# Mixing the second GLA pair's decay levels with its own value and gate projections, and moving half of a key load behind the first attention block

## The chip, the cores and the metric

One Trainium2 chip, one core of it. The metric is the device time of one execution in microseconds (us), median of several; lower is better. The engines are TensorE (PE), VectorE (DVE), ScalarE (ACT), GpSimd (POOL) and SyncE (SP), which issues nearly all DMAs here. "Clock" is the share of full speed that the chip granted to TensorE.

## The reference, cut to what matters

One layer for 1024 tokens of width 1024: an FFN, a mixer, an FFN, each with a residual and a layer norm. The mixer is what the change touches. It projects the tokens once and splits the columns into head groups:

```python
proj = h @ w_in
gq, gk, gv, gg, ga, dq, dk, dv, iq, ik, iw = jnp.split(proj, offs, axis=-1)
...
log_a = (jax.nn.log_sigmoid((ga @ w_gla_a2 + b_gla_a)) / GLA_TAU)
o = gla_chunked(q, k, v, log_a)          # 4 heads, linear attention with decay
o = o * lax.rsqrt(jnp.mean(o * o, axis=-1, keepdims=True) + RMS_EPS) * gla_norm_g
o_gla = o.reshape(B, T, GLA_WIDTH) * jax.nn.silu(gg)
o_dsa = dsa_attention(dq, dk, dv, iq, ik, iw)   # 8 heads, the 256 best keys of an index score
return jnp.concatenate([o_gla, o_dsa], axis=-1) @ w_out
```

In `gla_chunked` each step multiplies a running state by `exp` of a cumulated decay, adds `k^T v`, and reads it with `q`. In `dsa_attention` an index score picks, for each query, at most 256 of the keys before it; softmax attention runs over those.

## The kernel before, in words

The FFNs take most of the time and stay as they are. Each float32 matmul of a projection is three fast ones (high times high, low times high, high times low), so one projection block of 128x512 is 24 matmuls: 3 for each of 8 slices of the width.

**The GLA pairs.** The four GLA heads are worked on in two pairs by the generator `gla_pair` (L868 to L1052), which gives control back after each piece of work. A pair first makes `pz`, the decay's logits (two halves of 512 tokens), takes log-sigmoid of them on ACT and DVE (`az`, `kz`, the tiles `mz` are the tiles `kz`), and cumulates along 128-token blocks with scans on DVE (`bT`, L898). Then, for each half `i` of the tokens, it computes the state of the blocks (`turned_keys`: `pk`, `kt`; `pkv`, then `state`) and the scores inside a block by levels L = 0, 64, 32, ... 1 (L957): level 0 is the diagonal (`qk = gk*gq` on POOL into `kz[1]`, L964, then `pd` on PE); every other level builds `ee` (DVE, then Abs and Exp on ACT), `kz` (POOL) and `qz` (DVE), a small product `pa` on PE (L995), and copies it into `at` through a mask on DVE (L1006). `po` = `at` times values plus `qe` times state closes the half; `og` is `po` with norm and gate, and goes to DRAM.

**Its inputs.** `gla_items(p)` projects `gq`, `gk` (4 blocks of 24 matmuls, tile `pf`) and `gv`, `gg` (8 token blocks, tile `pt`, by `proj_tok`), takes silu of the gate and multiplies it by the norm's weights (`gg*gn`, L1452, on POOL). `dq_steps` projects the queries of the other attention: two halves of the tokens by four units; after each unit `stage_split` (L1393) splits the block into a high and a low part (`part`, ACT and DVE) and sends both to DRAM (`q_hi`, `q_lo`).

**Order.** Inside `in_order()` the PE instructions stand as the code writes them; all other engines are ordered by the framework's scheduler, which moves work up. Before the change, pair 1's `gq`, `gk`, `gv` and `gg` blocks all run in one piece between the first `pz` and the levels, and only the queries' steps are mixed with the levels, three steps (9 matmuls) a level.

**The search and the attention.** While this goes on, DVE is ending the search for the 256th key and turns scores into biases (`search_keys`, L781; `keep_keys`, L816 to L848). The tiles that hold the split tokens of the first half are then overwritten by the keys: `kst` (`xl`, `xh`), eight DMAs of 512 KB (L1525), and the values `vt` (L1526). They can start only once the queries of the first half (i = 0) have been projected. Queries come back from DRAM into `qq` and `ql` (`load_q`, L1063). `attend` starts with three `lg` (logits, L1091); `rb` (L1150) closes a 128-token block. `Weights.need` brings weights ahead, RING = 6 of them.

Of the kernel before, what the change touches and what calls it, by code (L numbers as in the profile page):

```python
# [7 lines left out]
F32 = mybir.dt.float32  # L8
# [107 lines left out]
class Block:  # L116
# [542 lines left out]

    def proj_tok(self, u, b, xT):  # L660

        nc = self.nc
        cols = slice((b % 4) * P, (b % 4) * P + P)
        xh, xl = xT[0][b // 4], xT[1][b // 4]
        pt = self.ps_pj.tile([P, 512], F32, tag="pj", name=self.uid("pt"))
        for k in range(KD):
            wh, wl = self.w.get(u + k // 2)
            nc.tensor.matmul(pt, xh[:, k, cols], wh[:, k % 2, :], start=(k == 0), stop=False)  # L668
            nc.tensor.matmul(pt, xh[:, k, cols], wl[:, k % 2, :], start=False, stop=False)  # L669
            nc.tensor.matmul(pt, xl[:, k, cols], wh[:, k % 2, :], start=False, stop=(k == KD - 1))  # L670
        return pt

# [199 lines left out]
    def gla_pair(self, p, g, gp, go, sgp, ps, masks, consts, o_dram):  # L872
# [32 lines left out]
                )  # L905
        yield
        gq, gk, gv, gg = g[p]
        ebl = gp.tile([P, NB], F32, tag="ebl", name=self.uid("ebl"), bufs=2)
        nc.scalar.activation(ebl, bT.rearrange("p (b t) -> p b t", t=P)[:, :, P - 1], AF.Exp, scale=1.0 / 16)

# [17 lines left out]
            nc.scalar.activation(kt, pk, AF.Copy)  # L928
            return kt

        kt = turned_keys(0)
        yield
        state = None
        for i in range(2):
            ts = slice(i * HT, (i + 1) * HT)
            last = NB - 1 - 4 * i
            pkv = self.ps_tp.tile([P, 4, P], F32, tag="tp", name=self.uid("pkv"))
            for j in range(min(4, last)):
                for h in range(2):
# [1 line left out]
                    nc.tensor.matmul(  # L941
                        pkv[rows, j, :], kt[:, j, rows], gv[:, 4 * i + j, h * P : (h + 1) * P], start=True, stop=True
                    )
            states = [state]
            for j in range(min(4, last)):
                b = 4 * i + j
                new = gp.tile([P, P], F32, tag="state", name=self.uid("state"), bufs=5)
                if b == 0:
                    V.tensor_copy(new, pkv[:, j, :])
                else:  # L950
                    V.scalar_tensor_tensor(new, state, ebl[:, b : b + 1], pkv[:, j, :], ALU.mult, ALU.add)
                state = new
                states.append(new)
            yield
            at = go.tile([P, 4, 2, P], F32, tag="at", name=self.uid("at"), bufs=1)
            for step, L in enumerate((0, 64, 32, 16, 8, 4, 2, 1)):
                if L == 8:  # L957
                    eb = gp.tile([P, HT], F32, tag="ee", name=self.uid("eb"), bufs=2)
                    nc.scalar.activation(eb, bT[:, ts], AF.Exp, scale=1.0 / 16)
                    V.tensor_mul(qe[0][:HP], gq[:HP, ts], eb[:HP])  # L960
                    nc.gpsimd.tensor_mul(qe[1][HP:], gq[HP:, ts], eb[HP:])
# [40 lines left out]
                for h in range(2):  # L1002
                    if L == HP:
                        nc.scalar.activation(at[:HP, :, h, HP:], pa[h][:HP], AF.Copy)
                    else:
# [2 lines left out]
                            masks[L].unsqueeze(1).to_broadcast([P, 4, HP // L, L]),  # L1008
                            pa[h].rearrange("p a (n l) -> p a n l", l=L),
                        )  # L1010
                yield
            if i == 0:
                kt = turned_keys(1)
                yield
            if p == 1 and i == 1:
                po = [self.ps_pj.tile([P, 4, P], F32, tag="pj", name=self.uid("po")) for _ in range(2)]
# [159 lines left out]
    def run(self):  # L1176
# [160 lines left out]
        with ExitStack() as s2:  # L1337
# [8 lines left out]
            with ExitStack() as s3:  # L1346
# [84 lines left out]
                def gla_items(p):  # L1431
                    gq = gqk.tile([P, T], F32, tag="gq", name=f"gq{p}", bufs=1)
                    gk = gqk.tile([P, T], F32, tag="gk", name=f"gk{p}", bufs=1)
                    for dst, u, sc in ((gq, um["gq", p], 0.125), (gk, um["gk", p], 1.0)):
                        self.w.need(u, u)
                        for i in range(2):
                            pt = self.proj_feat(u, i, x1T)
                            nc.scalar.activation(dst[:, i * HT : (i + 1) * HT], pt, AF.Copy, scale=sc)
                            yield
                    gv = go.tile([P, NB, 256], F32, tag="gv", name=f"gv{p}", bufs=1)  # L1440
                    gg = go.tile([P, NB, 256], F32, tag="gg", name=f"gg{p}", bufs=1)
                    u = um["gvg", p]
                    self.w.need(u, u + 3)
                    for b in range(NB):
                        pt = self.proj_tok(u, b, x1T)
                        nc.scalar.activation(gv[:, b, :], pt[:, 0:256], AF.Copy)
                        nc.scalar.activation(gg[:, b, :], pt[:, 256:512], AF.Copy)
                        yield
                    nc.scalar.activation(gg, gg, AF.Silu)
                    for b in range(0, NB, 2):  # L1450
                        gv2 = gg[:, b : b + 2, :].rearrange("p b (h f) -> p (b h) f", h=2)
                        nc.gpsimd.tensor_mul(gv2, gv2, gn.unsqueeze(1).to_broadcast([P, 4, P]))  # L1452
                    g_in[p] = (gq, gk, gv, gg)

                def dv_items():
                    u = um["dv"]
# [7 lines left out]
                def dq_steps():  # L1464
                    for i in range(2):
                        for t, u in enumerate(um["dq"]):
                            for pt in self.proj_steps(u, i, x1T):
                                yield
                            stage_split(pt, q_dram, t, i)

                def gla(p):
                    return self.gla_pair(p, g_in, gp, go, sgp, ps, masks, consts, og_dram)

                for _ in gla_items(0):
                    pass
                self.interleave(dv_items(), gla(0), 3)
                items = gla_items(1)
                for _ in range(4):
                    next(items)
                side = gla(1)  # L1480
                next(side)
                for _ in items:
                    pass
                self.w.need(um["dq"][0], um["dq"][3])
                fill = dq_steps()
                half = (3, 2) + (3,) * 7
                with self.in_order():
                    for n in (3, *half, 3, 0, 0, 0, 0, *half):
                        next(side)
                        for _ in range(n):  # L1490
                            next(fill)
                    for _ in fill:
                        pass
                    for _ in side:
                        pass
                found = self.search_keys(scores, bp, tkp, tp)
                for b in scores:
                    bias[b] = self.keep_keys(
# [17 lines left out]
                qp.append((qq, ql))  # L1516
                self.load_q(i, q_dram, qp[i])
            vt = [p.tile([P, 4, 512], F32, name=f"vt{i}") for i, p in enumerate((vp0, vp))]
            for i in range(2):
                cs = slice(i * HT, (i + 1) * HT)  # L1520
                for e in range(2):
                    for j in range(2):
                        r0 = 64 * (e ^ j)
                        src = k_dram[i][j].rearrange("(q e d) t -> e d q t", e=2, d=64)
                        nc.sync.dma_start(kst[e][r0 : r0 + 64, :, cs].bitcast(F32), src[e])  # L1525
                nc.sync.dma_start(vt[i], dv_dram[i].rearrange("(b t) f -> t b f", t=P))  # L1526
            c0 = self.new_half(1)
            cat = []
            with tc.tile_pool(name="ps_att", bufs=1, space=PSUM, reuse_waits="tile") as ps:
                def begin(b):  # L1530
                    c = catp.tile([P, D], F32, tag="cat", name=self.uid("cat"))
                    cat.append(c)
                    nc.sync.dma_start(c[:, 0:512], og_dram[b * P : (b + 1) * P, :])
                    return c

                def end(b, c):
                    if b < 4:
                        self.split_cat(c, b, [[c0[0]], [c0[1]]])
                    if 0 < b < 5:
                        if b == 1:  # L1540
                            self.w.need(um["out"][0], um["out"][0] + 3)
                        half = x1_dram[(b - 1) * P : b * P, 0:512]
                        xh = scores[NB - 1][:, 512:]
                        nc.sync.dma_start(xh, half)
                        pt = self.proj_tok(um["out"][0], b - 1, [[c0[0]], [c0[1]]])
                        nc.vector.scalar_tensor_tensor(xh, xh, ALPHA, pt, ALU.mult, ALU.add)
                        nc.sync.dma_start(half, xh)

                self.attend(kst, vt, bias, q_dram, qp, ep, tp, rp, ps, begin, end)
# [114 lines left out]
```

## Time and profile before

| | before |
|---|---|
| median of 3 runs | 2028.18 us (2027.34 to 2028.61) |
| profiled execution | 2028.19 us, of which span 2026.1 us |
| PE busy | 1957.7 us (97%) |
| DVE, ACT, POOL busy | 1474.1, 823.0, 594.3 us (73, 41, 29%) |
| clock, mean | 0.985 |

The span is first to last instruction; the profiled execution's time has 2.1 us around it. PE is busy nearly always, so what can be won are its few gaps and its stretches at a low clock. The work that the change moves lies between 970 and 1150 us.

### The profile page before, as it was taken

What the parts mean: (1) busy time and instruction counts of PE and PEld (TensorE: products, weight loads), DVE (VectorE), ACT (ScalarE), POOL (GpSimd) and SP (SyncE); (2) the same over time, 40 slices, a digit from 0 to 9 for tenths busy, and PEclk for the clock granted to TensorE, in tenths of its full rate; (3) what the DMA queues carried; (4) which work ended last, traced back from release to release, by engine and by line L of the source; (5) the groups of instructions that cost most, each with busy time, mean ns of one, the idle gap of its engine ahead of it and who ended that gap; (6) DMA issues with size and microseconds to landing.
All of it is one profiled execution on the core that took longest, in us unless ns stands there. A gap on an engine that the chain in (4) does not pass through costs nothing.

```text
span 2026.1 us, 26935 instructions
## 1 busy us (share of the span) xinstructions
PE 1957.7 (97%) x9752; PEld 1608.2 (79%) x9752; DVE 1474.1 (73%) x2326; ACT 823.0 (41%) x1319; POOL 594.3 (29%) x503
## 2 busy tenths in 40 slices
PE   8999999999999999999988899999999999999997
PEld 6888888888888788777766678787888888888886
DVE  5577778785668767899974457576677877866577
ACT  4333332334333454798433346333333233234331
POOL 3345445440001102144253000044444544420011
PEclk9999999999999999999988899999999999999999
DMA  5345445469656332021127621432453454487664
GB/s 176 115 141 188 147 144 182 155 207 331 193 181 205 105 93 84 22 63 57 49 68 174 171 72 38 141 133 71 145 176 132 160 183 136 156 288 264 207 194 149
DMA packets 192708, 298.43 MB, mean 147 GB/s; under 512 B 16304, under 2 KB 98368, under 8 KB 192576
## 3 DMA queue, kind: packets, MB, share of 16 engines
q1 hardware_dynamic: 192576, 296.72, 45.2%
q8 instruction: 76, 1.25, 0.3%
q14 instruction: 56, 0.46, 0.1%
HBM read 205.96 MB, written 90.70 MB: 146 GB/s over the span
## 4 chain that ended last, share of the span: by engine, by line
PE 80%; DVE 8%; issue 3%; DMA 3%; ACT 2%; POOL 2%; SPq 1%; POOLq 0%; DVEq 0%; ACTq 0%
PE pd L491 19%; PE pq L320 14%; PE pq L321 14%; PE pq L319 14%; DVE junk L781 3%; PE pf L655 3%; PE pf L656 3%; PE pf L657 2%; PE pv L1134 2%; PE tpe L1118 2%; PE pt L668 1%; PE pt L670 1%; PE pt L669 1%; PE tp L265 1%; POOL wlo L75 1%
## 5 line engine op out<-in xcount | busy, mean ns | idle before, releaser
L97 DVE TENSOR_TENSOR wloq<-rw,whiq 128x512 fp32r<-128x512 f32 (+1 forms) x208 | 213.9, 1031 | 113.2 <-ACT whiq L96 112.2
L97 DVE TENSOR_TENSOR wlod<-rd,whid 128x1024 fp32r<-128x1024 f32 x154 | 186.2, 1219 | 127.2 <-ACT whid L96 126.6
L96 ACT ACTIVATE whid<-rd 128x1024 fp32r<-128x1024 f32 x154 | 160.9, 1058 | 242.5 <-PE pd L491 170.9
L96 ACT ACTIVATE whiq<-rw 128x512 fp32r<-128x512 f32 (+1 forms) x208 | 163.5, 806 | 227.3 <-POOL rw L305 95.6
L491 PE MATMUL pd<-wlod,whid 128*128 128x512 f32 x616 | 239.7, 389 | 0.8 <-DVE wlod L97 0.8
L491 PE MATMUL pd<-whid,wlod 128*128 128x512 f32 x616 | 239.2, 389 | 0.0
L491 PE MATMUL pd<-whid 128*128 128x512 f32 x616 | 234.7, 390 | 0.0
L319 PE MATMUL pq<-b_h,whiq 128*128 128x512 f32 x576 | 228.7, 397 | 1.9 <-ACT b_h L96 1.9
L320 PE MATMUL pq<-b_l,whiq 128*128 128x512 f32 x576 | 225.0, 391 | 1.2 <-DVE b_l L97 1.2
L321 PE MATMUL pq<-b_h,wloq 128*128 128x512 f32 x576 | 224.8, 391 | 0.0
L207 POOL TENSOR_TENSOR rs<-ve,neghalf 128x1 f32<-128x1 f32 x24 | 33.8, 1410 | 609.4 <-DVE ve L225 609.4
L431 ACT ACTIVATE c<-c 128x512 f32<-128x512 f32 x80 | 50.5, 632 | 236.5 <-DVE c L355 134.5
L319 PE MATMUL pq<-xh,whiq 128*128 128x512 f32 x352 | 137.7, 391 | 0.0
L321 PE MATMUL pq<-xh,wloq 128*128 128x512 f32 x352 | 137.0, 389 | 0.0
L320 PE MATMUL pq<-xl,whiq 128*128 128x512 f32 x352 | 136.9, 389 | 0.0
L491 PEld LDWEIGHTS pd<-wlod,whid 128*128 128x128 f32 x616 | 115.7, 188 | 25.4 <-DVE wlod L97 1.6
L491 PEld LDWEIGHTS pd<-whid,wlod 128*128 128x128 f32 x616 | 115.6, 188 | 24.2
L491 PEld LDWEIGHTS pd<-whid 128*128 128x128 f32 x616 | 115.6, 188 | 23.8 <-ACT whid L96 0.4
L668 PE MATMUL pt<-whi,xh 128*128 128x512 f32 x320 | 129.6, 405 | 4.4 <-ACT stage L1460 2.4
L319 PEld LDWEIGHTS pq<-b_h,whiq 128*128 128x128 f32 x576 | 108.6, 189 | 23.8 <-ACT b_h L96 2.5
L320 PEld LDWEIGHTS pq<-b_l,whiq 128*128 128x128 f32 x576 | 108.7, 189 | 23.2 <-DVE b_l L97 2.1
L669 PE MATMUL pt<-wlo,xh 128*128 128x512 f32 x320 | 126.8, 397 | 0.0
(263 smaller groups left out, 4498.4 us busy)
## 6 DMA issues: line engine op xcount, KB each, us to landing
rw<-in_ffn_w_gu_dram SPq DMA_DIRECT2D x88, 512.0 KB, 4.2
rd<-h_dram SPq DMA_DIRECT2D x154, 256.0 KB, 3.4
h_dram<-c SPq DMA_DIRECT2D x148, 256.0 KB, 3.0
rt<-in_ffn_w_down_dram SPq DMA_DIRECT2D x44, 512.0 KB, 3.5
t_dram<-rt SPq DMA_DIRECT2D x44, 512.0 KB, 3.0
rd<-t_dram SPq DMA_DIRECT2D x88, 256.0 KB, 3.8
rd<-in_ffn_w_down_dram SPq DMA_DIRECT2D x66, 256.0 KB, 3.8
raw<-in_w_in_dram SPq DMA_DIRECT2D x20, 512.0 KB, 3.8
```

The source lines that it names most:

```text
L96: self.nc.scalar.activation(hi, src, AF.Copy)
L97: self.nc.vector.tensor_sub(lo, src, hi)
L319: mm(bank, wh[:, k, :], xh[:, k, :], start=(start and k == 0), stop=False)
L320: mm(bank, wh[:, k, :], xl[:, k, :], start=False, stop=False)
L321: mm(bank, wl[:, k, :], xh[:, k, :], start=False, stop=(stop and k == 3))
L431: nc.scalar.activation(t, t, AF.Silu)
L491: nc.tensor.matmul(bank, left, right, start=(i == 0 and n == 0), stop=(i == ng - 1 and n == 2))
L655: nc.tensor.matmul(pt[:m], wh[:, k, :m], xh[:, k, :], start=(k == 0), stop=False)
L656: nc.tensor.matmul(pt[:m], wh[:, k, :m], xl[:, k, :], start=False, stop=False)
L668: nc.tensor.matmul(pt, xh[:, k, cols], wh[:, k % 2, :], start=(k == 0), stop=False)
L669: nc.tensor.matmul(pt, xh[:, k, cols], wl[:, k % 2, :], start=False, stop=False)
L781: V.tensor_scalar(junk[:, :n], scores[b], thr, None, ALU.is_ge, ALU.add, accum_out=cnt)
```

## The change

Six edits:
1. `proj_tok` becomes a generator `tok_steps` that gives control back after each of the 8 slices. The 8 `gvg` blocks of pair 1 become 64 steps that stand ahead of the queries' 64 steps in one list of filler; the levels take 14 steps, then 6 each (second half: 7 each), and what is left (8 steps, the last unit of the queries) comes behind the last `po`.
2. In pair 1 the keys are turned at level 4 and the states made at level 2 of each half, not ahead of the levels.
3. `gv`/`gg` weights come with a shorter ring (4), and those of the queries one by one.
4. `gg*gn` of pair 1 goes from POOL to DVE.
5. Weights of the output projection are asked for at the start of block 0 of the attention rather than at the end of block 1.
6. The second half of keys and values is loaded in `begin` of block 1 (`load_keys(1)`), not ahead of the attention.

```diff
+    def tok_steps(self, u, b, xT):
...
-        return pt
+            yield pt
...
-        kt = turned_keys(0)
-        yield
-        state = None
+        for i in range(2):
+            ts = slice(i * HT, (i + 1) * HT)
+            if not p:
+                kt = turned_keys(i)
+                yield
+                states_of(i, kt)
+                yield
             for step, L in enumerate((0, 64, 32, 16, 8, 4, 2, 1)):
+                if p and L == 4:
+                    kt = turned_keys(i)
...
+                if p and L == 2:
+                    states_of(i, kt)
                 yield
...
-                    self.w.need(u, u + 3)
+                    self.w.need(u, u + 3, RING - 2 * p)
                     for b in range(NB):
-                        pt = self.proj_tok(u, b, x1T)
+                        if p and b in (4, 6):
+                            self.w.need(u + b // 2 + 2, u + b // 2 + 2, 1)
+                        for k, pt in enumerate(self.tok_steps(u, b, x1T)):
+                            if k < KD - 1:
+                                yield
...
-                        nc.gpsimd.tensor_mul(gv2, gv2, gn.unsqueeze(1).to_broadcast([P, 4, P]))
+                        (nc.vector if p else nc.gpsimd).tensor_mul(gv2, gv2, gn.unsqueeze(1).to_broadcast([P, 4, P]))
...
+                side = gla(1)
+                next(side)
                 items = gla_items(1)
                 for _ in range(4):
                     next(items)
-                side = gla(1)
-                next(side)
-                for _ in items:
-                    pass
-                self.w.need(um["dq"][0], um["dq"][3])
-                fill = dq_steps()
-                half = (3, 2) + (3,) * 7
+                def fill():
+                    yield from items
+                    yield from dq_steps()
+                fill = fill()
                 with self.in_order():
-                    for n in (3, *half, 3, 0, 0, 0, 0, *half):
+                    for n in (14,) + (6,) * 7 + (8, 0, 0, 0) + (7,) * 8:
                         next(side)
                         for _ in range(n):
                             next(fill)
-                    for _ in fill:
-                        pass
                     for _ in side:
                         pass
+                for _ in fill:
+                    pass
...
+            load_keys(0)
...
+                    if b == 0:
+                        self.w.need(um["out"][0], um["out"][0] + 3)
+                    if b == 1:
+                        load_keys(1)
```

How it moves instructions, at three places. On PE at the start of pair 1 before the change: behind the two `pz` follow 192 `pt` matmuls and then `pk`, `pkv` and `pd`; `pf` are queries here.

```order
L882 MATMUL pz_7881<-mT,wa_5343 128x512
L882 MATMUL pz_7885<-mT,wa_5343 128x512
L668 MATMUL pt_7914<-whi_7726,xh_3620 128x512
L669 MATMUL pt_7914<-wlo_7727,xh_3620 128x512
L670 MATMUL pt_7914<-whi_7726,xl_3621 128x512
L668 MATMUL pt_7914<-whi_7726,xh_3620 128x512
```

The same place after the change; `pf_7879` is the last block of `gk`, and `pt_7915` the first of the eight value and gate blocks.

```order
L655 MATMUL pf_7879<-xh_3622,whi_7042 128x512
L656 MATMUL pf_7879<-xl_3623,whi_7042 128x512
L657 MATMUL pf_7879<-xh_3622,wlo_7043 128x512
L886 MATMUL pz_7730<-mT,wa_5343 128x512
L977 MATMUL pd_7909<-heads,kz_6648 128x2 x4
L672 MATMUL pt_7915<-whi_7753,xh_3620 128x512
L673 MATMUL pt_7915<-wlo_7754,xh_3620 128x512
L674 MATMUL pt_7915<-whi_7753,xl_3621 128x512
```

The diagonal product `pd`, which reads `kz_6648`, now stands directly behind the second `pz`, and every `pt` behind it.

On DVE at the end of `keep_keys` before the change: the last rows of the last block (`score_6535`) stand together, and the states and the diagonal follow.

```order
L821 SCALAR_TENSOR_TENSOR keep_9528<-keep_9528,left_9532 128x1024
L822 TENSOR_SCALAR keep_9528<-score_6535,search_8875 128x1024
L823 TENSOR_TENSOR keep_9528<-keep_9528 128x1024
L825 TENSOR_SCALAR score_6535<-keep_9528 128x1024
L920 TENSOR_TENSOR mT<-bT_7878 128x512
L949 COPY state_8201<-pkv_8192 128x128
```

The same place after the change: level work of the first half stands between, down to the masked copies of level 1 (`mask_101`), which are the last that the first `po` needs.

```order
L826 TENSOR_SCALAR keep_9510<-score_6535,search_8857 128x1024
L1016 COPY_PREDICATED at_8347<-mask_105,pa_8172 128x4x32x2
L827 TENSOR_TENSOR keep_9510<-keep_9510 128x1024
L1016 COPY_PREDICATED at_8347<-mask_105,pa_8173 128x4x32x2
L999 TENSOR_TENSOR qz_6645<-gq_7748,ee_8441 128x256
L829 TENSOR_SCALAR score_6535<-keep_9510 128x1024
L951 COPY state_8193<-pkv_8184 128x128
L991 TENSOR_TENSOR ee_8487<-bT_7723 128x512
L953 SCALAR_TENSOR_TENSOR state_8195<-state_8193,ebl_7905,pkv_8184 128x128
L953 SCALAR_TENSOR_TENSOR state_8197<-state_8195,ebl_7905,pkv_8184 128x128
L953 SCALAR_TENSOR_TENSOR state_8199<-state_8197,ebl_7905,pkv_8184 128x128
L1016 COPY_PREDICATED at_8347<-mask_101,pa_8237 128x4x64
```

So the whole first half's level work moved up among the rows of `keep_keys`.

On SP after the change, at the key loads (`k_hi_85` and `k_lo_86` are the first half of the tokens, `k_hi_87` and `k_lo_88` the second; `q_hi_83` is the first part of the second half's queries):

```order
L1545 DMA xh_9560<-k_lo_86 64x4x512
L1545 DMA xl_9561<-k_lo_86 64x4x512
L1545 DMA xh_9560<-k_hi_87 64x4x512
L1545 DMA xh_9560<-k_lo_88 64x4x512
L1545 DMA xl_9561<-k_hi_87 64x4x512
L1546 DMA vt_9578<-dv_dram_89 128x4x512
L1545 DMA xl_9561<-k_lo_88 64x4x512
L1407 DMA q_hi_83<-part_8625 128x512
L1407 DMA q_lo_84<-part_8626 128x512
L1072 DMA qq_9562<-q_hi_81 64x8x128
L1073 DMA ql_9563<-q_lo_82 64x4x128
```

All eight key loads still stand ahead of the first `qq` and `ql`, as they did before the change. The first `vt`, which stood behind that `ql`, now stands among them.

## Rows read from the trace of the kernel before

**Rows 1.** The page: its first line, and the chain that ended last.

```profile
span 2026.1 us, 26935 instructions
...
PE 80%; DVE 8%; issue 3%; DMA 3%; ACT 2%; POOL 2%; SPq 1%; POOLq 0%; DVEq 0%; ACTq 0%
```

**Rows 2.** Busy time by stretch: length, PE, PEld, DVE, ACT, POOL, clock, DMA share, GB/s.

```profile
1000.00:1040.00 40.00, 38.80 (x187) 31.28 (x185) 39.15 (x58) 15.55 (x27) 13.08 (x12) 1.00 0.03 8
1040.00:1050.00 10.00, 0.83 (x12) 0.50 (x12) 4.29 (x7) 3.75 (x5) 10.00 (x11) 0.68 0.45 157
1050.00:1076.00 26.00, 26.00 (x182) 20.47 (x180) 16.39 (x29) 11.27 (x20) 11.64 (x14) 0.93 0.24 82
...
1122.00:1146.00 24.00, 14.75 (x77) 11.74 (x77) 9.80 (x48) 9.32 (x41) 3.06 (x4) 0.72 0.59 167
```

**Rows 3.** PE's timeline: start, length, instruction, idle time before it and its releaser.

```profile
974.60 0.61 PE L1027 MATMUL po<-state,qe 128*128 128x128 f32 x4
...
984.71 1.98 PE L882 MATMUL pz<-mT,wa 16*128 16x512 f32 x4
...
1049.50 1.12 PE L995 MATMUL pa<-qz,kz 64*64 64x64 f32 x16 [9.17 <-POOL kz L988]
...
1076.37 0.39 PE L657 MATMUL pf<-xh,wlo 128*128 128x512 f32 x1
...
1103.07 0.79 PE L655 MATMUL pf<-xh,whi 128*128 128x512 f32 x1 [5.70 <-DVE part L1396]
...
1121.94 0.28 PE L1091 MATMUL lg<-xh,qq 128*128 128x256 f32 x1
...
1124.87 0.49 PE L1024 MATMUL po<-gv,at 128*128 128x128 f32 x2 [2.06 <-DVE part L1396]
...
1136.86 0.55 PE L1091 MATMUL lg<-xh,qq 128*128 128x256 f32 x1 [4.37 <-DVE mx L1095]
...
1146.25 1.07 PE L1150 MATMUL rb<-ident,rc 128*64 128x128 f32 x8
```

**Rows 4.** Timelines of DVE, POOL and ACT around pair 1's setup.

```profile
995.99 2.62 DVE L898 TENSOR_TENSOR_SCAN bT<-onesf,kz 128x128 f32<-128x128 f32 x8
...
1039.46 1.77 DVE L920 TENSOR_TENSOR mT<-bT 128x512 f32<-128x512 f32 x1
...
998.76 1.32 POOL L964 TENSOR_TENSOR kz<-gk,gq 128x512 f32<-128x512 f32 x1 [9.14 <-DVE bT L898]
...
1039.22 5.59 POOL L1452 TENSOR_TENSOR gg<-gg,gn 128x512 f32<-128x512 f32 x4
...
988.47 1.28 ACT L895 ACT_TABLE_LOAD   x1
```

**Rows 5.** DVE's groups of instructions, 1050 to 1100: busy, mean ns, idle before.

```profile
L1006 DVE COPY_PREDICATED at<-mask,pa 128x256 f32<-128x256 uint8 x14 | 6.5, 532 | 3.8 <-PE pa L995 3.8
L981 DVE TENSOR_TENSOR ee<-bT 128x512 f32<-128x512 f32 x9 | 6.2, 691 | 3.8 <-POOL qe L961 2.0 <-POOL kz L988 1.2
L989 DVE TENSOR_TENSOR qz<-gq,ee 128x256 f32<-128x256 f32 x9 | 5.1, 564 | 0.5 <-ACT ee L983 0.5
...
L960 DVE TENSOR_TENSOR qe<-gq,eb 64x512 f32<-64x512 f32 x2 | 1.9, 947 | 4.1 <-ACT eb L959 4.1
L970 DVE TENSOR_TENSOR at<-ident,pd 128x1024 f32<-128x1024 f32 x1 | 1.2, 1207 | 0.0
L951 DVE SCALAR_TENSOR_TENSOR state<-state,ebl,pkv 128x128 f32<-128x128 f32 x3 | 1.0, 346 | 7.0 <-PE pkv L941 7.0
```

**Rows 6.** The DMA view, 1070 to 1150: GB/s in 2-us slices.

```profile
GB/s 143 131 0 0 202 205 208 204 212 204 208 205 199 212 279 296 197 281 361 249 108 270 296 202 151 191 199 158 275 91 0 0 124 82 234 191 270 377 294 197
```

**Rows 7.** SP's issues of the first key load and a `q_hi`; ACT's wait for its landing.

```profile
1076.57 0.67 SPq L1525 DMA_DIRECT2D xl<-k_hi  x1
...
1083.38 0.33 SPq L1398 DMA_DIRECT2D q_hi<-part  x1
...
1100.93 0.60 ACT L1395 ACTIVATE part<-pf 128x512 fp32r<-128x512 f32 x1 [9.48 <-DMA q_hi<-part]
```

More of the change, by code (lines that the diff above doesn't have):

```diff
@@ L660, in proj_tok @@
     def proj_tok(self, u, b, xT):
+        return list(self.tok_steps(u, b, xT))[-1]
+    def tok_steps(self, u, b, xT):
         nc = self.nc
@@ L907, in gla_pair @@
         gq, gk, gv, gg = g[p]
+        states = [None]
         ebl = gp.tile([P, NB], F32, tag="ebl", name=self.uid("ebl"), bufs=2)
@@ L929, in turned_keys, with states_of @@
             return kt
-        kt = turned_keys(0)
-        yield
-        state = None
-        for i in range(2):
-            ts = slice(i * HT, (i + 1) * HT)
+        def states_of(i, kt):
             last = NB - 1 - 4 * i
@@ L943, in gla_pair @@
                     )
-            states = [state]
+            del states[:-1]
             for j in range(min(4, last)):
@@ L950, in gla_pair @@
                 else:
-                    V.scalar_tensor_tensor(new, state, ebl[:, b : b + 1], pkv[:, j, :], ALU.mult, ALU.add)
-                state = new
+                    V.scalar_tensor_tensor(new, states[-1], ebl[:, b : b + 1], pkv[:, j, :], ALU.mult, ALU.add)
                 states.append(new)
-            yield
+        for i in range(2):
[5 more added lines that the diff above has]
+                yield
             at = go.tile([P, 4, 2, P], F32, tag="at", name=self.uid("at"), bufs=1)
             for step, L in enumerate((0, 64, 32, 16, 8, 4, 2, 1)):
+                if p and L == 4:
+                    kt = turned_keys(i)
                 if L == 8:
@@ L1010, in gla_pair @@
                         )
-                yield
-            if i == 0:
-                kt = turned_keys(1)
+                if p and L == 2:
+                    states_of(i, kt)
                 yield
@@ L1433, in gla_items @@
                     gk = gqk.tile([P, T], F32, tag="gk", name=f"gk{p}", bufs=1)
+                    gv = go.tile([P, NB, 256], F32, tag="gv", name=f"gv{p}", bufs=1)
+                    gg = go.tile([P, NB, 256], F32, tag="gg", name=f"gg{p}", bufs=1)
+                    g_in[p] = (gq, gk, gv, gg)
                     for dst, u, sc in ((gq, um["gq", p], 0.125), (gk, um["gk", p], 1.0)):
@@ L1439, in gla_items @@
                             yield
-                    gv = go.tile([P, NB, 256], F32, tag="gv", name=f"gv{p}", bufs=1)
-                    gg = go.tile([P, NB, 256], F32, tag="gg", name=f"gg{p}", bufs=1)
                     u = um["gvg", p]
-                    self.w.need(u, u + 3)
+                    self.w.need(u, u + 3, RING - 2 * p)
                     for b in range(NB):
-                        pt = self.proj_tok(u, b, x1T)
+                        if p and b in (4, 6):
[3 more added lines that the diff above has]
+                                yield
                         nc.scalar.activation(gv[:, b, :], pt[:, 0:256], AF.Copy)
                         nc.scalar.activation(gg[:, b, :], pt[:, 256:512], AF.Copy)
-                        yield
+                        if b < NB - 1:
+                            yield
                     nc.scalar.activation(gg, gg, AF.Silu)
@@ L1451, in gla_items @@
                         gv2 = gg[:, b : b + 2, :].rearrange("p b (h f) -> p (b h) f", h=2)
-                        nc.gpsimd.tensor_mul(gv2, gv2, gn.unsqueeze(1).to_broadcast([P, 4, P]))
-                    g_in[p] = (gq, gk, gv, gg)
+                        (nc.vector if p else nc.gpsimd).tensor_mul(gv2, gv2, gn.unsqueeze(1).to_broadcast([P, 4, P]))
+                    yield
                 def dv_items():
@@ L1466, in dq_steps @@
                         for t, u in enumerate(um["dq"]):
-                            for pt in self.proj_steps(u, i, x1T):
-                                yield
+                            for k, pt in enumerate(self.proj_steps(u, i, x1T)):
+                                if i == 0 and t < 2 and k == 3:
+                                    self.w.need(um["dq"][t + 2], um["dq"][t + 2], 1)
+                                if k < KD - 1:
+                                    yield
                             stage_split(pt, q_dram, t, i)
+                            yield
                 def gla(p):
@@ L1518, in run, with load_keys @@
             vt = [p.tile([P, 4, 512], F32, name=f"vt{i}") for i, p in enumerate((vp0, vp))]
-            for i in range(2):
+            def load_keys(i):
                 cs = slice(i * HT, (i + 1) * HT)
@@ L1539, in end @@
                     if 0 < b < 5:
-                        if b == 1:
-                            self.w.need(um["out"][0], um["out"][0] + 3)
                         half = x1_dram[(b - 1) * P : b * P, 0:512]
```

## The prediction

> **What bounds the kernel now.** I read the page's chain first: PE makes 80% of it, DVE 8% [rows 1]. So a change pays only by closing a gap of PE or a stretch at a low clock. The stretches come next [rows 2]: from 1000 to 1040 PE is busy 38.80 of 40 us at full clock while DVE is busy 39.15; from 1040 to 1050 PE does 0.83 us of work; from 1122 to 1146 it does 14.75 us of 24 at clock 0.72. DVE's 39.15 is the biasing of scores plus a little of the pair's work, and the reader should see that both engines are full there at once. PE's timeline names the gaps [rows 3]: 9.17 us before 1049.50 on a `kz` from POOL, which ran `gg*gn` for 5.59 us just ahead [rows 4]; 5.70 us before 1103.07; 2.06 and 4.37 us in the attention's start. The 5.70 us is a `part` whose buffer had to land in DRAM first: ACT waited 9.48 us for it [rows 7].
>
> Four marks carry the sum. T1, the end of the first half's queries, is 1076.37+0.39 less the 0.39's pipelined tail, about 1076.4 [rows 3]; the first key load starts at 1076.57, right behind it [rows 7]. The first `lg` is at 1121.94 and the first `rb` at 1146.25 [rows 3]. Behind `rb` I change nothing, so the time moves as `rb` moves.
>
> **Edits 1 and 2, the start of pair 1.** Before, PE had 192 `pt` matmuls of cover between `pz` and `pd`. The order rows show `pd` directly behind the second `pz` now, with all `pt` behind it. `pd` needs `kz[1]` = gk*gq, and that tile is still read by the second half's scans (`mz` is `kz`). Before, the scans ended at 995.99+2.62 = 998.61 and POOL's product ran from 998.76 to 1000.08 [rows 4]. In the new order, ahead of those scans DVE loses most of the biasing of the 512-wide block (about 4.5 us) and gains one `mT`, `ee` and `qz` (1.77 [rows 4], 0.69 and 0.56 [rows 5]): about 997. The path by ACT is no shorter: the second `pz` must now wait for the `og` of pair 0 that frees its PSUM bank, and Abs, Exp and Ln follow, with table loads of 1.28 us [rows 4]. I take 997.7 for the scans and 999 for `kz`.
>
> PE's previous work ends much earlier. `po` of pair 0 ends at about 975 [rows 3]; from there to `pz` at 984.71 stand 42 projections, 0.23 us each. Now 27 stand between the two `pz`, the other 15 ahead of `po`, where PE had short waits, so it is through at about 982.4. It then idles some 16 us until 999, but for one `pz`. A stall like this costs afterwards too: behind the 9.17 us, 1050 to 1076 ran at a mean clock of 0.93, so 0.07 x 26 = 1.8 us [rows 2].
>
> From 999 PE needs 0.5 (`pd`), 42 projections (9.5), seven levels of 18 projections and `pa` (7 x (4.1+1.1) = 36.4), and the 1.8 us of clock: it could be at the first `po` at about 1048 (1047.2 plus `pk` and `pkv`, which partly overlap).
>
> **The same edits on DVE.** `po` needs the masked copies of level 1, and the order puts these behind nearly all of `keep_keys`. DVE was full until 1039.46, when `keep_keys` ended [rows 4]. Moved in front of that point are seven `ee` (4.8), six `qz` (3.4), twelve masked copies (6.4), `at` 1.2, a `qe` 0.9, one `mT` 1.8 and four states (1.4) [rows 4, 5]: 19.9 us. Durations listed overlap by about 0.08 us each (1.5 to 2.6 us in all), POOL's 1039.22 row and its neighbours no longer run against the last of `keep_keys` (I give 2.4 us for that, an estimate, since the 1024-wide rows there are longer than the 896-wide ones by more than the width), and I add 1 us that DVE waits for ACT. 1039.5 + 19.9 - 2.3 - 2.4 + 1 = 1055.7; I take 1055, with bounds 1051 (more overlap) and 1058 (none of the relief). PE idles 7 us here, and pays perhaps 3 us of clock behind it (1.8 as above, and an estimate of as much again at most).
>
> **Where T1 falls.** From the first `po` to T1 PE has 120 projections (27.2), `po` 3.6, `pd` 0.8 and `pa` 3.8: 35.4. With 3 of clock and about 2 for `part` and `og` behind POOL's `grs`, T1 = 1055 + 40.4 = 1095, 19 us later than before. Part of that is work brought forward: PE then needs only 20.6 us more to the first `lg`, 1116 by PE alone, 6 us earlier than before. That is what the removed gaps (9.17 + 5.70 + 2.06) and the block moved behind `lg` (5.4) pay, less the new ones.
>
> **Edit 6 and what comes after T1.** By the order, nothing of the key loads has moved behind the first queries: eight stand ahead of `qq` and `ql` as before, and the first `vt` joined them. Keys move at about 205 GB/s (the slices from 1078 to 1098 [rows 6]): 8 x 0.524 = 4.19 MB, 20.5 us. Behind them come `vt` (1.05 MB), four query parts (1.05) and `qq`, `ql` (0.79): 2.89 MB at some 270 GB/s (the slices 1098 to 1108 [rows 6]), 10.7. With 2 us of issue and landing the first `lg` can't start before T1 + 33 = 1128, and PE idles 12 us ahead of it. Before, this gate was hidden, because PE had 45.5 us of work and waits between T1 and `lg` [rows 3]. That the queue passes them in order shows in rows 7: a `q_hi` issued at 1083.38 behind the eight keys let ACT go only at 1100.93, 17.6 us later.
>
> The Trainium skill ("DMA: Bandwidth & Descriptors", section "Queues, rings and completion order") says that completion is not FIFO per issuing engine, although each DMA engine consumes its ring in order. By that alone a later `ql` could land ahead of a key; the trace shows the opposite for this queue (the 17.6 us), and I forecast by the trace.
>
> **The attention's start.** From `lg` to `rb` it took 24.3 us [rows 3]. Off go 2.06 and 4.37, whose `part` and `og` are done by now under the gate; on comes the last query unit (5.4 at full clock, up to 10 at half, and this stretch had 0.72). 24.3 - 6.4 + 7.5 = 25.4. `rb` at 1128 + 25.4 = 1153.4, 7.2 us later than 1146.25.
>
> **Edits 3, 4, 5.** Weights in a shorter ring: covered by 16 steps of filler; nothing. `gg*gn` on DVE: 4 x 0.69 = 2.8 us, behind level 1, where DVE had 9.6 us idle in 26 [rows 2]; nothing on the path, and POOL is free of 5.59. If that cover fails, T1 is 2.8 later. Output weights earlier: three DMAs behind `ql`; nothing for `lg`. The gate could grow by 2 if they went ahead.
>
> **The sum.** 2028.19 (the profiled execution; the median is 2028.18) + 7.2 = 2035.4; I say 2035. Less than 0.2% (4.1 us) either way can't be told from no change here.
>
> **Rivals.**
> - *The gate isn't there* (faster): `qq` and `ql` land before PE gets to `lg`, because they pass the keys or because keys move faster when nothing else does. Then `lg` is at 1116 and `rb` at 1140 to 1141.5: 2022 to 2023.5. It decides as soon as `ql` lands by T1 + 21. Against it: 20.5 us for the keys alone. 0.15, with a sooner T1 too. The rule of the Trainium skill named above would allow such passing, and by it the time would be this one.
> - *The two new stalls are smaller* (same): level 1 on DVE ends at 1051, no `part` wait, little clock: T1 = 1089, `lg` 1122, `rb` 1147.5: 2029.5. For it: DVE durations are mixtures; against: both engines were full already. 0.27.
> - *Longer* (slower still): DVE at 1058, the last query unit at half clock, and its bank waiting for `og`: `rb` 1159, 2041. 0.13.
> - *The second half's load moves nothing*: this is what the order shows, and it is in my case. If the change had truly put it behind `qq`, the gate would be T1 + 23, `lg` 1118: 2025.
>
> My case has 0.45, its own range 2031 to 2039. A quarter of it lies within 4.1 us of before. Slower: three quarters of 0.45 + 0.13 + little of the second = 0.50; same 0.33; faster 0.17 (the first rival and a little). For 8 in 10 I leave out most of the first rival's lower part and the last's tail: 2023 to 2041.
>
> **What would show it.** On PE: `pd` (L977) waits for POOL some 10 us or more before 999; the first `po` (L1033) of pair 1 waits 4 to 9 us for a DVE masked copy near 1055; the 9.17 and 5.70 us waits are gone; `lg` (L1100) waits about 12 us for a DMA near 1128, within 33 us of T1. DVE is full from 985 to 1055. The clock dips behind each gap. Wrong would be: `lg` not ended by a DMA, T1 before 1089, or `rb` before 1147.

## The result, and the profile after

The changed kernel takes 2042.73 us (median of 4, 2039.10 to 2045.01), the kernel before 2027.76 us (median of 4 with one run more). The ratio is 1.0075, 95% interval 1.0056 to 1.0094: slower, by about twice what was forecast and 1.7 us above the top of the range.

The page of the changed kernel, its first line and its chain, beside [rows 1]:

```profile
span 2040.0 us, 26930 instructions
...
PE 75%; DVE 11%; DMA 5%; issue 3%; POOL 2%; ACT 2%; SPq 1%; POOLq 0%; DVEq 0%; ACTq 0%
```

PE's share of the chain fell from 80 to 75%, and DMA's rose from 3 to 5. The span grew by 13.9 us. Busy time by stretch, columns as in [rows 2], of the changed kernel:

```profile
985.00:1000.00 15.00, 1.81 (x7) 0.98 (x6) 14.41 (x33) 10.12 (x14) 9.01 (x8) 0.62 0.26 70
1000.00:1040.00 40.00, 40.00 (x229) 32.10 (x230) 39.40 (x68) 11.85 (x24) 8.06 (x7) 0.93 0.00 1
1040.00:1050.00 10.00, 10.00 (x75) 8.18 (x74) 9.96 (x15) 2.44 (x5) 3.19 (x3) 1.00 0.03 3
1050.00:1076.00 26.00, 23.02 (x119) 19.19 (x118) 11.99 (x22) 15.33 (x35) 13.86 (x16) 0.87 0.20 62
...
1122.00:1146.00 24.00, 15.17 (x72) 12.85 (x73) 6.28 (x28) 6.99 (x28) 3.05 (x4) 0.72 0.79 216
1146.00:1164.00 18.00, 9.45 (x61) 6.99 (x61) 9.28 (x36) 6.79 (x24) 0.00 (x0) 0.77 0.87 236
```

and the last of these stretches in the kernel before:

```profile
1146.00:1164.00 18.00, 17.18 (x122) 13.32 (x122) 10.15 (x38) 8.14 (x25) 0.00 (x0) 0.90 0.68 158
```

Four things are to be seen. PE stands from 985 to 1000. The 10 us from 1040 to 1050, empty before [rows 2], are full now, so the old stall is gone. From 1122 to 1146 PE's work and clock have hardly changed. And from 1146 to 1164, a stretch of which the forecast said nothing, PE does 9.45 us of work instead of 17.18, at a lower clock.

PE's timeline of the changed kernel, its long waits in order, beside [rows 3]:

```profile
999.07 1.87 PE L977 MATMUL pd<-heads,kz 128*128 128x2 f32 x8 [13.19 <-POOL kz L974]
...
1054.31 1.15 PE L1033 MATMUL po<-gv,at 128*128 128x128 f32 x3 [2.98 <-DVE at L1016]
...
1127.84 0.55 PE L1100 MATMUL lg<-xh,qq 128*128 128x256 f32 x1 [10.08 <-DMA qq<-q_hi]
...
1137.94 0.50 PE L655 MATMUL pf<-xh,whi 128*128 128x512 f32 x1 [1.74 <-DVE og L1049]
...
1151.57 0.29 PE L1159 MATMUL rb<-ident,rc 128*64 128x128 f32 x1
...
1160.06 1.09 PE L194 MATMUL tp<-ident,cat 128*128 128x128 f32 x4 [7.29 <-DMA cat<-og_dram]
```

SP's issues of the changed kernel around the last wait, and the first key load (T1):

```profile
1095.98 0.67 SPq L1545 DMA_DIRECT2D xl<-k_hi  x1
...
1146.78 0.57 SPq L1073 DMA_DIRECT2D ql<-q_lo  x1
1147.45 0.55 SPq L1407 DMA_DIRECT2D q_hi<-part  x1
1148.09 0.38 SPq L279 DMA_DIRECT2D rw<-in_ffn_w_gu_dram  x1
1148.57 0.58 SPq L1072 DMA_DIRECT2D qq<-q_hi  x1
1149.24 0.57 SPq L1407 DMA_DIRECT2D q_lo<-part  x1
1149.86 0.58 SPq L1072 DMA_DIRECT2D qq<-q_hi  x1
1150.54 0.67 SPq L1073 DMA_DIRECT2D ql<-q_lo  x1
1151.26 10.24 SPq L1555 DMA_DIRECT2D cat<-og_dram  x5
```

The same queue of the kernel before, where `cat` came ahead of block 2's queries:

```profile
1139.67 0.60 SPq L1526 DMA_DIRECT2D vt<-dv_dram  x1
1140.32 0.98 SPq L1533 DMA_DIRECT2D cat<-og_dram  x2
1141.34 0.59 SPq L1063 DMA_DIRECT2D qq<-q_hi  x1
```

PE's first use of that `cat` in the kernel before, and the load in the changed kernel's chain of work that ended last:

```profile
1148.59 1.04 PE L194 MATMUL tp<-ident,cat 128*128 128x128 f32 x4 [0.42 <-DMA cat<-og_dram]
```

```profile
1151.26 8.67 DMA cat<-og_dram
```

From its issue to its first use `cat` took nearly as long before, 8.3 us against 8.8. What differs is the moment of issue: 5.9 us ahead of the first `rb` before, 0.3 us ahead after.

The second `rb`, before and after:

```profile
1163.37 0.27 PE L1150 MATMUL rb<-ident,rc 128*64 128x128 f32 x1
```

```profile
1177.28 0.27 PE L1159 MATMUL rb<-ident,rc 128*64 128x128 f32 x1
```

From these rows the loss can be followed mark by mark (us, the profiled executions; the last row is the `rb` of the second block):

| mark | before | after | after less before |
|---|---|---|---|
| T1, first key load | 1076.57 | 1095.98 | +19.4 |
| first `lg` | 1121.94 | 1127.84 | +5.9 |
| first `rb` | 1146.25 | 1151.57 | +5.3 |
| second `rb` | 1163.37 | 1177.28 | +13.9 |
| end of span | 2026.1 | 2040.0 | +13.9 |

Up to the first `rb` the change costs 5.3 us; between the first and the second `rb` another 8.6, and behind that nothing. Of the 8.6, 6.9 are the longer wait for `cat` (7.29 less 0.42); the other 1.7 were not taken apart (the clock from 1146 to 1164 is 0.77 instead of 0.90).

### The profile page after: what moved, and what is told of

Read it like the earlier page. It is cut to its first block, busy times and chain, and to the rows that moved or that the text cites. A ratio compares the mean times of both kernels' runs of the same rounds, so it can differ in the third digit from the quotient of the medians.

```text
span 2040.0 us, 26930 instructions
## 1 busy us (share of the span) xinstructions
PE 1958.7 (96%) x9752; PEld 1608.2 (79%) x9752; DVE 1475.2 (72%) x2330; ACT 823.8 (40%) x1321; POOL 587.6 (29%) x499
## 3 DMA queue, kind: packets, MB, share of 16 engines
q8 instruction: 76, 1.25, 0.3%
## 4 chain that ended last, share of the span: by engine, by line
PE 75%; DVE 11%; DMA 5%; issue 3%; POOL 2%; ACT 2%; SPq 1%; POOLq 0%; DVEq 0%; ACTq 0%
PE pd L491 18%; PE pq L319 12%; PE pq L321 12%; PE pq L320 12%; DVE junk L785 3%; PE pf L655 2%; PE pf L656 2%; PE pf L657 2%; PE pv L1143 2%; PE tpe L1127 2%; PE pt L672 2%; PE pt L673 1%; PE pt L674 1%; PE tp L265 1%; DVE ee L991 1%
## 5 line engine op out<-in xcount | busy, mean ns | idle before, releaser
L674 PE MATMUL pt<-whi,xl 128*128 128x512 f32 x320 | 127.6, 400 | 0.0
L319 PEld LDWEIGHTS pq<-b_h,whiq 128*128 128x128 f32 x576 | 108.5, 188 | 23.7 <-ACT b_h L96 2.7
```

Source lines behind the costliest of these rows:

```text
L319: mm(bank, wh[:, k, :], xh[:, k, :], start=(start and k == 0), stop=False)
```

## The experiments

**Theory Q**, formed on these rows: the 8.6 us are a DMA wait. Ahead of `cat` (the 256 KB of `og` rows that block 0 needs) SP now has block 2's query loads, the last query unit's stores and the first FFN2 weight load, because that unit now runs inside the attention's start. **Rival O**: `cat` is late because the key gate makes `og` itself late. The rest of the loss was to be the two stalls and the gate of the prediction. In all, twelve kernels; the ratio is that to the kernel before, run beside each, whose median lies between 2026.76 and 2027.90 us. Runs of different sets are better compared by their ratios than by their times.

**1. The last query unit back ahead of the last `po`.**

```diff
-                    for n in (14,) + (6,) * 7 + (8, 0, 0, 0) + (7,) * 8:
+                    for n in (14,) + (6,) * 7 + (8, 0, 0, 0) + (8,) * 8:
```

> The last unit of the queries goes back ahead of the last po (8 steps a level in the second half of pair 1), so no projection block lies in the attention's start. Theory Q (the surplus of the change over the forecast, some 8.6 us, is the load of block 0's og rows into cat, which stands in SP's queue behind what the late query unit holds up): T1 near 1095.5 as after, the first lg still ended by the queries' DMA near 1128, first rb near 1146, cat awaited for under 1.5 us; time 2027 to 2031 us. Rival O (cat is late because the gate makes og itself late): the wait for cat stays at 6 us or more, time 2035 to 2038.

Measured: 2036.77 us, ratio 1.0050 (1.0037 to 1.0063). The wait for `cat` is gone, but the time is 6 us above what theory Q forecast. PE's waits in this run:

```profile
1129.58 0.55 PE L1100 MATMUL lg<-xh,qq 128*128 128x256 f32 x1 [4.45 <-issue]
1134.17 0.79 PE L1033 MATMUL po<-gv,at 128*128 128x128 f32 x2 [3.41 <-DVE part L1405]
...
1146.61 0.55 PE L1100 MATMUL lg<-xh,qq 128*128 128x256 f32 x1 [4.42 <-DVE mx L1104]
...
1152.89 0.55 PE L1100 MATMUL lg<-xh,qq 128*128 128x256 f32 x1 [1.73 <-DMA qq<-q_hi]
...
1156.25 2.12 PE L1159 MATMUL rb<-ident,rc 128*64 128x128 f32 x16
1158.31 0.93 PE L194 MATMUL tp<-ident,cat 128*128 128x128 f32 x4
```

`tp` starts right behind `rb`, with no wait: `cat` stands ahead of block 2's queries again and is issued at 1149.41, 6.8 us ahead of `rb`. But `lg` to `rb` now takes 26.7 us, 2.9 more than in the changed kernel, although the unit's 7.2 us of work are gone from there. PE waits 3.41 us for a `part` that frees the bank of `po`, 4.42 us for `mx` and 1.73 us for queries. The kernel before has these three waits too (2.06, 4.37 [rows 3] and 1.58); in the changed kernel they are gone, and PE has the query unit to do there. So Q is right on `cat`, and my forecast for this run forgot what the unit had covered in the attention's start.

**2. Only the queue mended: the stores by POOL, and block 2's queries and the FFN2 weight behind `cat`.**

```diff
-                        nc.sync.dma_start(dst[i][j][t * P : (t + 1) * P, :], part[j].bitcast(F32))
+                        q = nc.gpsimd if dst is q_dram and (t, i) == (3, 1) else nc.sync
+                        q.dma_start(dst[i][j][t * P : (t + 1) * P, :], part[j].bitcast(F32))
...
+                if b == 2:
+                    self.tc.add_manual_dep(
+                        nc.cur_bb.bb.instructions[-1],
+                        self.first_cat.name,
...
```

> The late query unit stays in the attention's start. Only the queue changes: its two stores go out by POOL's queue, and block 2's query loads and the first FFN2 weight load stand behind block 0's cat load on SP. Theory Q: cat is issued near 1144.5, 6 to 7 us earlier, PE waits under 2 us for it; 2034 to 2037. Rival O (og itself is late): PE still waits 6 us or more for cat; 2041 to 2044.

The FFN2 weight load has the same edge, which these lines leave out.

Measured: 2032.79 us, 1.0034 (1.0021 to 1.0046), some 8 us below the changed kernel by the ratios and a little below the range forecast. SP's issue of `cat`, and PE:

```profile
1146.44 9.42 SPq L1573 DMA_DIRECT2D cat<-og_dram  x2
```

```profile
1154.00 0.29 PE L1176 MATMUL rb<-ident,rc 128*64 128x128 f32 x1
...
1155.13 0.66 PE L194 MATMUL tp<-ident,cat 128*128 128x128 f32 x4
...
1171.26 0.27 PE L1176 MATMUL rb<-ident,rc 128*64 128x128 f32 x1
```

No wait for `cat`, which is issued 7.6 us ahead of `rb` here; first to second `rb` is 17.3 us (1171.26 less 1154.00), against 25.7 after and 17.1 before. The edit leaves `og` where it was (its last stores begin 42 us behind T1 in both kernels), so rival O falls.

**3. The two halves of that edit, apart.** The stores alone:

> Of the run with cat first, the part that sends the late query unit's two stores by POOL's queue, alone; block 2's query loads stay ahead of cat on SP, and those wait for the end of block 0's logits. If the stores alone held cat up: cat issued near 1145, time 2034 to 2037. If the query loads behind which cat stands hold it as well: cat issued near 1150, PE waits 5 us or more, time 2040 to 2043.

Measured: 2038.54 us, 1.0053 (1.0040 to 1.0066); `cat` was issued at 1149.80 and PE waited 7.74 us. Its first to second `rb` took 25.4 us, as in the changed kernel: with the stores out of SP's queue the loads still hold `cat` up, as the second case says. The time is below the 2040 to 2043 of that case (of the some 4 us that it is lower than the changed kernel's, 1.5 lie ahead of T1, at 1094.45; the rest stays open). The loads alone:

> The complement of the run with the stores alone: block 2's query loads and the first FFN2 weight load stand behind block 0's cat load, the late query unit's stores stay on SP ahead of it. If the stores by themselves hold cat up as long as their block takes: cat issued near 1149.5, PE waits 5 us or more, 2039 to 2042. If only the loads did: cat issued near 1144, wait under 2 us, 2033 to 2036.

Measured: 2032.59 us, 1.0025 (1.0016 to 1.0034). Neither expectation names what happened: `cat` was issued late, as the one said, and not waited for, as the other said. SP's queue and PE in this run:

```profile
1149.18 3.28 SPq L1572 DMA_DIRECT2D cat<-og_dram  x2
1152.56 0.58 SPq L1081 DMA_DIRECT2D qq<-q_hi  x1
...
1151.62 1.07 PE L1176 MATMUL rb<-ident,rc 128*64 128x128 f32 x15
1152.82 0.63 PE L194 MATMUL tp<-ident,cat 128*128 128x128 f32 x4
```

`cat` is issued 2.1 us earlier than after, and used by 1152.82, 3.6 us behind its issue. In the changed kernel it took 1151.26 to 1160.06, 8.8 us. So against the changed kernel it is the way through the queue that got shorter, more than the issue that came sooner; against the kernel before, where the way took 8.3 us, only the late issue is new. Both hang on what stands ahead of `cat` on SP: the loads ahead take SP's time to issue, and then they pass first. In the trace of the changed kernel all 39 transfers that SP issued from T1 up to this `cat` landed in the order of their issue.

**4. Only the weight left ahead of `cat`.** To tell bytes from kinds of load:

> As the run with the loads behind cat, but the first FFN2 weight load (512 KB) stays ahead of cat on SP; block 2's query loads (768 KB in six parts of 128 or 256 KB) stay behind it. If cat is late by the bytes that the queue has to pass ahead of it, at some 200 to 250 GB/s, the weight adds 2 to 2.6 us: PE waits 1 to 3 us for cat, time 2033 to 2037. If only the query loads hold it up: no wait, 2031 to 2034. If any one load ahead is enough: 5 us or more, 2039 to 2042.

Measured: 2035.77 us, 1.0038 (1.0024 to 1.0051), in the range of the first case. (Block 2's loads are four, two of 256 and two of 128 KB, not six.) SP's issue of `cat`, and PE:

```profile
1147.43 5.45 SPq L1565 DMA_DIRECT2D cat<-og_dram  x2
```

```profile
1153.53 0.63 PE L194 MATMUL tp<-ident,cat 128*128 128x128 f32 x4 [2.59 <-DMA cat<-og_dram]
```

PE used `cat` 6.1 us behind its issue, 2.5 us more than with only the stores ahead. For 512 KB that would be about 210 GB/s, so theory Q takes the form that `cat` is late by the bytes ahead of it. The price per byte isn't shown, though: each figure is from one execution, and in run 7, where SP's order is that of the changed kernel, `cat` took 6.5 us from issue to use instead of 8.8.

**5. Filler ahead of the diagonal product.**

```diff
+                    for _ in range(14):
+                        next(fill)
-                    for n in (14,) + (6,) * 7 + (8, 0, 0, 0) + (7,) * 8:
+                    for n in (0,) + (6,) * 7 + (8, 0, 0, 0) + (7,) * 8:
                         next(side)
```

> The 14 steps of filler that stand behind the diagonal product pd now stand ahead of it; nothing else is edited. If PE's stall before pd is what delays the rest (PE theory): stall 13.2 becomes about 4, first po of pair 1 near 1044, T1 near 1086, time 9 us below the changed kernel, 2033. If DVE bounds the first half (DVE theory): PE waits again at the first po for the masked copy of level 1, which stands ahead of only the last 6.5 us of keep_keys in this order: po near 1048, T1 near 1090, lg 6 us earlier, 2036 to 2038.

Measured: 2035.37 us, 1.0046 (1.0032 to 1.0059). The two waits of the first half in this run:

```profile
999.05 1.05 PE L977 MATMUL pd<-heads,kz 128*128 128x2 f32 x8 [3.26 <-POOL kz L974]
...
1046.94 1.36 PE L1033 MATMUL po<-gv,at 128*128 128x128 f32 x4 [5.50 <-DVE left L823]
```

9.9 us were taken from the wait at `pd`; the wait at `po` rose from 2.98 to 5.50, and `po` came 7.4 us earlier, T1 6.2 (1089.77). PE alone could have been at `po` at 1041.4, and a masked copy of DVE (L1016) ended beside the `left` that the profile names, at 1046.9. So DVE does bind the first half there, 1 us sooner than the DVE theory forecast. The gate moved along: `lg` waited 9.84 us, 31.6 behind T1, and `cat` was still awaited 8.53 us.

**6. The second half of the keys truly behind the first queries.**

```diff
+                        if i == 1:
+                            self.tc.add_manual_dep(
+                                nc.cur_bb.bb.instructions[-1],
+                                first_q.name,
...
```

> The second half of the keys is held in SP's order behind the first block's query loads, as edit 6 says in words. Gate theory (lg waits because eight key loads are ahead of qq and ql in the queue): first lg 8 to 10 us earlier than after, 1118 to 1120, within 24 us of T1; the time falls by as much as the wait for cat lets through, 2033 to 2037. Rival (the queries' own way through DRAM or SP's waits for part are the gate): lg stays within 3 us of 1128 and the time within 2 us of 2042.

Measured: 2036.65 us, 1.0049 (1.0037 to 1.0062). `lg` in this run:

```profile
1117.37 0.36 PE L1100 MATMUL lg<-xh,qq 128*128 128x256 f32 x1 [0.17 <-DMA ql<-q_lo]
```

10.5 us earlier, and 22 us behind T1 (1095.43). The gate theory holds. Part was lost again: from `lg` to `rb` it now takes 30.2 us instead of 23.7. `po` waits 4.35 us for `part`, and the late query unit takes 8.29 us for its 24 matmuls at a mean clock of 0.67 (7.19 us at 0.76 in the changed kernel). `cat` is still awaited 6.48 us.

**7. Edits 5 and 6 undone in the changed kernel.**

```diff
+            load_keys(1)
...
-                    if b == 0:
-                        self.w.need(um["out"][0], um["out"][0] + 3)
-                    if b == 1:
-                        load_keys(1)
...
+                        if b == 1:
+                            self.w.need(um["out"][0], um["out"][0] + 3)
```

> The changed kernel with edits 5 and 6 undone (output weights asked for at the end of block 1 again, all keys and values loaded in one piece ahead of the attention). SP's order comes out the same as in the changed kernel. If the order is all that counts, the time is that of the changed kernel, 2039 to 2045, lg again ended by the queries' DMA and cat awaited for 7 us. Rival (edits 5 or 6 bring the output weights into the attention's start and are the cause of the late cat): 2034 or less.

Measured: 2040.95 us, 1.0061 (1.0047 to 1.0076); `lg` at 1127.88 with 10.23 us of wait for `qq`, `cat` awaited 5.04. SP's transfers come in the same order there as in the changed kernel. Edits 5 and 6 neither cost nor gain anything that shows: as written they don't alter the queue.

**8. Three mends at once**: those of 2, 5 and 6.

> The changed kernel with three mends at once: 14 steps of filler ahead of pd, the second half of the keys behind the first block's query loads, and block 0's cat load ahead of what the late query unit holds up. If the new stall at pd, the key gate at lg and the wait for cat are the whole of the loss (theory Q with gate and DVE theory): T1 near 1089, lg near 1111, rb near 1140, no wait for cat, time 2022 to 2027, no more than 2 us from before. Rival (something else in the changed kernel costs as well, such as the longer levels or gg on DVE): over 2031.

Measured: 2023.50 us, 0.9978 (0.9969 to 0.9987). T1 at 1089.9, `lg` at 1111.80 with no wait, first `rb` at 1142.39, no wait for `cat`. So with these three places mended nothing is left of the loss. That it is some 4 us faster than before doesn't show a gain of the rest of the change: the key order alone gives the kernel before as much (0.9973, run 10).

**9. The kernel before with edit 4 alone** (`gg*gn` on DVE):

> The kernel before with edit 4 alone: gg*gn of pair 1 on DVE instead of POOL. If POOL's 5.59 us of gg is what the 9.17 us stall before the first pa consists of, the stall falls to 3 to 4 us and the time by 4 to 6: 2021 to 2024. Rival (DVE, full to 1041 there, pays it back, or the gate at lg takes it up): time within 1.5 us of before.

Measured: 2026.23 us, 0.9993 (0.9984 to 1.0001): no difference. The stall fell only from 9.17 to 6.67 us, because POOL then waited for ACT. POOL in this run:

```profile
1042.76 1.59 POOL L922 TENSOR_TENSOR mT<-gk,mT 128x512 f32<-128x512 f32 x1 [1.63 <-ACT mT L921]
1045.14 3.00 POOL L75 TENSOR_TENSOR wlo<-raw,whi 128x256 fp32r<-128x256 f32 x4 [0.80 <-ACT whi L72]
1048.10 0.72 POOL L988 TENSOR_TENSOR kz<-gk,ee 128x256 f32<-128x256 f32 x1
```

`kz` stands behind `mT` and a weight's low part (3.00 us) in POOL's order, and `mT` waits for ACT. I had expected POOL's 5.59 us to come off the stall whole; 2.5 us did.

**10. The kernel before with the keys truly split** (the ordering edge of 6), alone and with edit 4.

> The kernel before with nothing but the second half of the keys held in SP's order behind the first block's query loads. If the 5.70 us stall of before comes from a part buffer landing behind eight key loads, this alone gives most of what the run with edit 4 and the keys gave: 2019 to 2022. Rival (edit 4 and the keys are worth something only together): 2025 or more.

> The kernel before with edit 4 and with the second half of the keys held in SP's order behind the first block's query loads. If the 5.70 us stall of before is a part buffer that lands behind the eight key loads, it falls under 2 us here, and the low clock behind it goes too: time 2013 to 2019. Rival (the second half of the keys delays the query parts all the same, or PE then waits in the attention's start for og): 2020 to 2024, no better than edit 4 alone.

Measured: 2023.00 us, 0.9973 (0.9963 to 0.9983) alone, and 2019.81 us, 0.9960 (0.9948 to 0.9972) with edit 4, the fastest of all here and faster than both kernels. Both times lie about 1 us above the range expected, and the two intervals overlap, so that edit 4 adds anything to the keys isn't shown. The `part` buffer that made the 5.70 us stall [rows 3, 7], in the second of these:

```profile
1087.93 0.60 ACT L1395 ACTIVATE part<-pf 128x512 fp32r<-128x512 f32 x1 [1.86 <-DMA og_dram<-og]
```

ACT's wait fell from 9.48 to 1.86 us. PE still waits 3.16 us there, for a `qz` of DVE, and the low clock didn't go: 0.86 from 1098 to 1122, against 0.79 before.

## Why the prediction was wrong

**The start of pair 1** was right. Forecast: `kz` ready at 999, PE idle some 16 us with one `pz` in between; measured: `pd` at 999.07 behind 13.19 us. Two sub-steps were wrong without weight, since the end of the stall is what counts: PE was through with its projections at 984.7, not 982.4, and the second `pz` didn't wait for `og`, it ran at 984.76. Run 5 shows the place.

**DVE's bound** was right in place and size: `po` at 1055 forecast, 1054.31 measured, behind the masked copies of level 1. That it came within 1 us is partly luck: the 2.4 us of relief in that sum were an estimate, and the rows of `keep_keys` for the last block came out 1.3 us shorter in all (one scan even longer, 3.38 us against 2.70). PE came to it later than I said (1051.3, not 1048), so it idled 2.98 us there and not 7. Most of that lies right behind the stall: from `pd` to the first `pt` took 1.7 us instead of 0.5, and the 42 projections 12.0 instead of 9.5, with only 1.8 us allowed for the clock in all.

**T1** was forecast at 1095 and lies at 1095.98, 41.7 us behind that `po` (forecast 40.4).

**The gate** was forecast at T1 + 33, `lg` at 1128; measured 1127.84, 31.9 us behind T1, with PE idle 10.08 us instead of 12. Run 6 shows that the keys make it. The Trainium skill's rule on completion ("DMA: Bandwidth & Descriptors", section "Queues, rings and completion order": not FIFO per issuing engine) found no sign here either: `ql` did not pass the keys, nor did any other of the 39 transfers from T1 to `cat` pass one that was issued ahead of it.

**The attention's start** took 23.7 us from `lg` to `rb`, forecast 25.4; the waits of 2.06 and 4.37 us that the forecast struck out are gone.

**The step that failed** is the sentence "Behind `rb` I change nothing, so the time moves as `rb` moves." The sum up to `rb` gave +7.2 and measured +5.3; behind it came 8.6 us that the sum didn't have. The change puts the last query unit into the attention's start; its two stores, the FFN2 weight and block 2's query loads now stand ahead of block 0's `cat` in SP's order. Before, `cat` stood ahead of all of the queries' loads for block 2 and was issued 5.9 us ahead of `rb`; now it is 0.3 us, the load takes 8.7 us to land, and PE waits 7.29 us for it. I counted that unit's matmuls, and neither its DMAs nor the loads that were reordered around it. The order of SP's instructions, which I read down to the first `qq`, had this some twenty rows further on. Runs 2 and 3 show the cause: with the query loads and the weight behind `cat`, first to second `rb` falls from 25.7 to 17.3 us, and to 16.45 (1167.94 less 1151.49) where the stores stay ahead; in that run T1, `lg` and the first `rb` lie within 0.4 us of the changed kernel's.

Of the **rivals**, "the gate isn't there" and "smaller stalls" did not occur. That edit 6 moves nothing was right (run 7). What it would give if it did, 2025, was not: in run 6 `lg` came at 1117.37, as said (1118), but the attention's start was longer, `cat` was late, and the time was 2036.65. The chance of 0.5 for slower named the right side; the range ended 1.7 us too low.

## What to carry to other kernels

When work moves past a phase's start, follow every queue that it uses as far as the first use behind the new place, not to the first wait only: a load that nothing computes on yet can push back one that the next block needs, both in its issue and on its way. A change of the source that is meant to move a load may not move it in the queue; an ordering edge did here, and that edge alone made the kernel before faster (0.9973), where the whole change made it slower (1.0075). And taking away the work that stands ahead of a stall's releaser need not shorten the stall by as much: with POOL's 5.59 us gone, 2.5 us of the 9.17 went.

## What the runs showed of the hardware

The key loads, of 64 partitions each, ran near 205 GB/s; the slices right behind them on the same queue came to 280 to 296, and later ones to 361 [rows 6]. A 256 KB load (`cat`) that needed 3.6 us from issue to use with nothing newer than the stores ahead (run 3) needed 8.8 us behind five more loads of 1.25 MB together in the changed kernel, with a mean DMA share of 0.87 from 1146 to 1164. In run 7, in the same order, it needed 6.5 us, and in the kernel before, right behind a `vt` of 1 MB, 8.3. Transfers issued by SP landed in the order of issue, 39 of 39 from T1 to `cat` in the changed kernel. After the 13.19 us stall PE ran 11 projection matmuls at 0.43 us each instead of 0.23: the granted clock was 0.50 (the 1.2 GHz level) from 1000.8 to 1005.4, and 1.00 from 1005.6 on.
